# Layer 0 of a Fourier / attention transformer on one core: the gate product moved to the front, in step with a modulation that arrives in eight pieces

## The chip, the core and the metric

The kernel runs on one core of one Trainium2 chip. The metric is the device time of one execution, in microseconds. Before the change it is 1901.31 us, the median of three runs (1898.41 to 1903.77).

All weights are 32-bit floats in the chip's memory; nothing stays on the core from one execution to the next, so some 360 MB are read and written in each.

## The reference, cut to what matters

Two sequences of 256 tokens with 2048 features, `x` and `ctx`, go through two layers. The change touches only layer 0, the Fourier one, where both sequences are handled alike (in the kernel as 512 columns, 256 of each). For `x`:

```python
shift, scale, gate = split(silu(c) @ ada_w[0] + ada_b[0], 3)     # the modulation
h    = rmsnorm(x, norm_g[0]) * (1 + scale) + shift
u, z = split(h @ w_in, 2)                                        # 4096 features each
f    = fft2(u in 16 groups of 256, over tokens and within a group, ortho).real
f    = f @ w_mix[group]                                          # per group
y    = f * silu(z)                                               # gated
x    = x + gate * (y @ w_out[0])
```

For `ctx` it is the same with `c_ctx`. So there are three large products: the u product with its transforms, the z product (called the **gate product** here, since silu(z) gates f) and the **output product** y @ w_out. Layer 1 is windowed attention and a last norm; its code is the same before and after.

## The kernel before, in words

The program is written in a tile framework. Pools hand out buffers (`raw`: three of 1 MB for loaded weights; `ws`: six of 0.5 MB for split weights; `act`: 34 of 0.25 MB; eight PSUM banks of 128x512), and a scheduler fixes, at build time, the order of the instructions on each engine. On the chip each engine runs its own list in that order and waits for semaphores. Loads are issued mostly by SP, some by ScalarE (ACT) and GpSimd (POOL); a DMA issue stands in its engine's list like any instruction.

Every large product is made of three single-pass products: `split` (L59) writes the rounded high part of a 32-bit tile on ACT (L60) and the rest on VectorE (DVE, L61), and `mm3` (L72 to L75) multiplies high by high, high by low and low by high. A weight of 1 MB is loaded by `raw` (L43), split in two halves by `half_split` (L63), and used by `ws_split`'s caller.

Layer 0 has four stages:

1. **Modulation and projection** (to 140 us). `x2`, the tokens as rows, is loaded as four tiles `xn` (L152) and squared for the norm (L162). For each quarter `nb` of the features: the scale part of the modulation is made from four 1 MB tiles of `awp` in `ada_pe` (L176 to L180: four products 32x512 per tile, which leave partial sums in four strips) and `ada_fin` (L182: copy `rows`, L184; eight small products with `sel`, L187, that turn the strips into columns; L188). Behind it `xn` is normed and split (L212, L213) and projected on cosines and sines over the tokens (`dmat`; L215 to L221); `evac_hx` (L190) scales the result by the modulation and splits it into `hx`, 16 pairs. Then the shift part of the modulation comes the same way (L272 to L305), with the first Fourier group's loads, products (`u0_emit`) and `load_m(0)` placed among its tiles. The shift only enters the column of frequency 0 (`f0`, L299 to L304).
2. **Fourier groups** (to 369 us). For each of 16 groups g (L311): `load_u` (L119 to L136: weights folded by POOL at L122 and DVE at L123, then split into `wmh`, `wml`, `wph`, `wpl`), `load_m(g)` (L233 to L256: the mixing matrix `m`, loaded on ACT's queue, folded by two DVE sums, split, and ten products), 96 u products, closing products (L364) and `ft` (L369, L370). Results are written to memory as `fd`, by POOL, and by ACT in the last group. Group 0 has a side product `asp` (L340 to L350) and eight zero fills (L326).
3. **Gate product** (to 718 us). `make_hs` (L419) loads a 128-row piece of `xT` (the tokens as columns) by POOL and makes the modulated, normed h as a pair (L428, L429, L430). The first four of 32 column blocks run together (weights `wz0`), the others one by one with `wz`. `z_out` (L434) takes silu (L437) and multiplies into `y`, which has come back from `fd`. Then `next(ada)` runs one step of `ada_jobs` (L386): one tile `adw` of the modulations that are needed later, each by four to eight reductions of 512 columns on DVE (`tensor_tensor_reduce`, L400). The vector of the conditioning itself comes as `cb`, a broadcast of `crow`.
4. **Output product** (to 1057 us). 32 steps with `wo0` tiles; `y_split0` splits the next two y blocks; `evac0` (L488) adds to the residual; `ada_rate` sets how many steps of `ada` run per step.

## Time and profile before

| | |
|---|---|
| median of three runs | 1901.31 us (1898.41 to 1903.77) |
| the profiled execution | 1903.14 us |
| its span, first to last instruction | 1901.3 us |
| mean granted TensorE clock | 0.989 of full |
| TensorE busy | 1837.0 us |
| VectorE, ScalarE, GpSimd busy | 1390.1, 934.2, 236.8 us |
| memory read, written | 345.30 MB, 12.59 MB |

How to read the profile: it is one execution, and times in it count from the span's start. PE is TensorE, PEld its weight load, DVE VectorE, ACT ScalarE, POOL GpSimd, SP the engine that issues most loads. A row of the timeline has start, length, engine, line, operation, output and inputs by the program's names, shapes, count; in square brackets stands how long the engine was idle before it, and who released it. A row of the groups has count, busy time, mean ns of one, and the idle time before them. Matmuls overlap in the pipeline, so a row's length is longer than the distance to the next start; the distance is what counts. `PEclk` and "granted clock" are the share of full speed that TensorE was given.

### The profile page before, as it was taken

Reading aid. Unit: us, or ns where it says so; the run is one execution under the profiler, and the core shown is the slowest. Engines: PE = TensorE matmul, PEld = TensorE weight load, DVE = VectorE, ACT = ScalarE, POOL = GpSimd, SP = SyncE. Lnnn points to the kernel's source line nnn. Section 1 sums busy time; section 2 is a strip of 40 time slices with the busy share of each in tenths; the row PEclk is TensorE's granted clock in tenths of the full one; section 3 lists DMA queues with packets and bytes.
Section 4 is the critical chain, followed back from the end, with each engine's and each line's share of the span. In section 5 each row is a group of like instructions: output and inputs, shape, how many; then the busy total and the mean of one; then the engine's idle time right before and its main releaser. Section 6 shows DMA issues by size and latency. Waiting matters only on the chain.

```text
span 1901.3 us, 27470 instructions
## 1 busy us (share of the span) xinstructions
PE 1837.0 (97%) x10433; PEld 1585.3 (83%) x10433; DVE 1390.1 (73%) x2711; ACT 934.2 (49%) x1602; POOL 236.8 (12%) x206
## 2 busy tenths in 40 slices
PE   6879999999999999999999999999999999999997
PEld 4469999888888888888888787899989989998886
DVE  5468888788777779687985644787787777787455
ACT  3234444442222234223331434788788888887443
POOL 0033334200000000000000001102212220200001
PEclk9889999999999999999999999999999999999999
DMA  9955444646666555764577323333333333434543
GB/s 384 386 227 182 182 182 182 234 171 254 228 227 236 216 220 197 286 231 154 196 271 267 120 89 119 147 133 112 133 134 112 133 111 134 164 128 175 199 177 133
DMA packets 60532, 359.67 MB, mean 189 GB/s; under 512 B 7600, under 2 KB 7744, under 8 KB 25328
## 3 DMA queue, kind: packets, MB, share of 16 engines
q1 hardware_dynamic: 49104, 324.83, 46.1%
q0 software_dynamic: 6720, 25.34, 3.5%
q10 hardware_dynamic: 4576, 7.74, 1.1%
q8 instruction: 82, 1.34, 0.3%
q14 instruction: 50, 0.41, 0.1%
HBM read 345.30 MB, written 12.59 MB: 188 GB/s over the span
## 4 chain that ended last, share of the span: by engine, by line
PE 90%; DVE 4%; DMA 3%; issue 2%; ACT 2%; POOL 0%; ACTq 0%; POOLq 0%; DVEq 0%; SPq 0%
PE ps L74 26%; PE ps L75 26%; PE ps L73 26%; PE ps L813 3%; PE ps L828 2%; PE ps L827 2%; PE ps L794 1%; PE ps L793 1%; DMA raw<-in_awp 1%; PE ps L180 1%; DMA raw<-in_wu 1%; DVE wpl L61 1%; DMA dm<-in_dmat 0%; POOL wm L122 0%; DVE ml L61 0%
## 5 line engine op out<-in xcount | busy, mean ns | idle before, releaser
L61 DVE TENSOR_TENSOR wl<-raw,wh 128x1024 fp32r<-128x1024 f32 x333 | 423.7, 1275 | 286.7 <-ACT wh L60 284.3
L60 ACT CAST wh<-raw 128x1024 fp32r<-128x1024 f32 x333 | 349.4, 1051 | 565.4 <-PE ps L74 506.0
L74 PE MATMUL ps<-act,wh 128*128 128x512 f32 x1024 | 398.2, 389 | 0.0
L73 PE MATMUL ps<-act,wh 128*128 128x512 f32 x1024 | 394.0, 389 | 0.0
L75 PE MATMUL ps<-act,wl 128*128 128x512 f32 x1024 | 391.0, 389 | 0.0
L75 PEld LDWEIGHTS ps<-act,wl 128*128 128x128 f32 x1024 | 192.3, 188 | 39.8
L73 PEld LDWEIGHTS ps<-act,wh 128*128 128x128 f32 x1024 | 192.3, 188 | 39.8
L74 PEld LDWEIGHTS ps<-act,wh 128*128 128x128 f32 x1024 | 192.3, 188 | 39.7
L400 DVE CUSTOM_DVE_ANT_0 raw<-raw,cb 128x512 f32<-128x512 f32 x256 | 172.5, 688 | 19.8 <-DMA raw<-in_adw 15.9
L73 PE MATMUL ps<-h,wh 128*128 128x256 f32 x512 | 147.0, 287 | 0.0
L74 PE MATMUL ps<-h,wh 128*128 128x256 f32 x512 | 144.7, 283 | 0.0
L75 PE MATMUL ps<-h,wl 128*128 128x256 f32 x512 | 144.7, 283 | 0.0
L400 DVE CUSTOM_DVE_ANT_0 junk<-raw,cb 128x512 f32<-128x512 f32 x192 | 131.7, 686 | 14.2 <-ACT cb L392 7.9
L74 PE MATMUL ps<-wl,h 128*128 128x512 f32 x320 | 125.3, 391 | 1.5 <-DVE wl L61 1.5
L73 PE MATMUL ps<-wh,h 128*128 128x512 f32 x320 | 124.2, 396 | 0.4 <-ACT h L583 0.4
L75 PE MATMUL ps<-wh,h 128*128 128x512 f32 x320 | 124.5, 392 | 0.0
L122 POOL TENSOR_TENSOR wm<-raw 128x1016 f32<-128x1016 f32 x32 | 83.4, 2614 | 195.2 <-DMA raw<-in_wu 194.7
L795 DVE CUSTOM_DVE_ANT_0 ps<-ps,mask,nsink 128x512 f32<-128x512 f32 x128 | 92.0, 753 | 10.8 <-PE ps L794 10.4
L73 PEld LDWEIGHTS ps<-h,wh 128*128 128x128 f32 x512 | 97.2, 190 | 1.3
L798 ACT ACTIVATE p<-ps,mx 128x512 f32<-128x512 f32 x128 | 87.3, 687 | 21.4 <-DVE mx L795 20.4
L74 PEld LDWEIGHTS ps<-h,wh 128*128 128x128 f32 x512 | 97.4, 190 | 0.0
L75 PEld LDWEIGHTS ps<-h,wl 128*128 128x128 f32 x512 | 97.3, 190 | 0.0
(302 smaller groups left out, 3775.6 us busy)
## 6 DMA issues: line engine op xcount, KB each, us to landing
raw<-in_wz SPq DMA_DIRECT2D x64, 1024.0 KB, 4.8
raw<-in_adw SPq DMA_DIRECT2D x64, 1024.0 KB, 4.8
raw<-in_awp SPq DMA_DIRECT2D x32, 1024.0 KB, 9.2
raw<-in_wo SPq DMA_DIRECT2D x32, 1024.0 KB, 6.0
raw<-in_wq SPq DMA_DIRECT2D x32, 1024.0 KB, 4.8
raw<-in_wu SPq DMA_DIRECT2D x32, 1016.0 KB, 4.9
raw<-in_wo1b SPq DMA_DIRECT2D x16, 1024.0 KB, 4.8
act<-in_xT POOLq DMA_DIRECT2D x32, 256.0 KB, 5.3
```

Of the source, the lines that this page charges most:

```text
L60: S.copy(h, src)
L61: V.tensor_tensor(l, src, h.bitcast(F32), op=ALU.subtract)
L73: PE.matmul(o, wh, xh, start=start, stop=False)
L74: PE.matmul(o, wh, xl, start=False, stop=False)
L75: PE.matmul(o, wl, xh, start=False, stop=stop)
L122: GP.tensor_tensor(m, v[:, :, 0, :], v[:, :, 1, :], op=ALU.subtract)
L400: V.tensor_tensor_reduce(junk if s == 0 and i < 3 else wf, wf, cb[:, s, kq * 512 : kq * 512 + 512], 1.0, 0.0, ALU.mult, ALU.add, acc[:, i, ...
L795: V.tensor_tensor_reduce(o, o, mask[:, tb, :], -0.125, nsink[:, i : i + 1], ALU.add, ALU.min, mx[:, tb : tb + 1])
L798: S.activation(pt[:, tb, :], so[tb], AF.Exp, bias=mx[:, tb : tb + 1], scale=-1.0, accum_out=sm[:, tb : tb + 1])
L813: PE.transpose(o[:, (kt * 2 + tb) * P : (kt * 2 + tb + 1) * P], pt[:, tb, c : c + P], ident)
L827: PE.matmul(oo[:, 0:N], st, ph[:, q], start=kb == 0, stop=False)
L828: PE.matmul(oo[:, 0:N], st, pl[:, q], start=False, stop=kb == 3)
```

## The change

It reorders layer 0, and regroups some of its operations.

- `xT` is loaded first, as four tiles of 1 MB that stay. The norm's sums of squares come from ACT squares and products with ones.
- Scale and shift arrive in eight pieces of 256 features. `ada_tile` loads half the rows of one piece for one of the two (two transfers of 512 KB, in runs of 1 KB) and makes eight products 32x256. `ada_fin` finishes both at once.
- As soon as piece c is there, `make_hs` makes h for its two row blocks k, and seven gate blocks (`NZ`, in seven PSUM banks) accumulate over them; the four tiles of piece c+1 stand between these products.
- The other 25 gate blocks follow one by one. `z_out` only takes silu and writes the block to memory as `zd`. Behind blocks 12, 16, 20 and 24 stands one quarter of the projection (`dft`), whose scaled result stays as `dfx`; 32 of the 64 `ada` steps are placed here, with reductions of 1024 columns.
- Behind the last block: `hx` is split from `dfx`, then come the casts and loads for group 0 with its `load_m(0)` and zero fills, and 16 Fourier groups as before.
- In the output product `y_split0` loads `fd` and `zd`, multiplies them and splits; `ada_rate` is lower.

```diff
+NZ = 7
...
+    def make_hs(k, xt):
+        h, l = act(F32R), act(F32R)
+        for s in range(2):
+            q = slice(s * N, (s + 1) * N)
+            t = xt[:, q]
+            V.scalar_tensor_tensor(t, t, gs0[:, k, s : s + 1], r_bc[:, q], op0=ALU.mult, op1=ALU.mult)
+            S.activation(h[:, q], t, AF.Identity, bias=sh0[:, k, s : s + 1])
+            V.scalar_tensor_tensor(l[:, q], t, sh0[:, k, s : s + 1], h[:, q].bitcast(F32), op0=ALU.add, op1=ALU.subtract)
+        hs.append((h, l))
...
+        xts = [st.tile([P, D], F32, name=f"xt{i}") for i in range(4)]
+        for i in range(4):
+            nc.sync.dma_start(xts[i], a["xT"][:, i * 4 : (i + 1) * 4, :])
...
+        for i in range(4):
+            sq = st.tile([P, D], F32, tag="raw2", name="sq", bufs=2)
+            S.activation(sq, xts[i], AF.Square)
+            for j in range(4):
+                PE.matmul(o[j * 32 : (j + 1) * 32, :], ones32, sq[:, j * 512 : (j + 1) * 512], start=i == 0, stop=i == 3)
...
+        bcast_rows(rr, r_bc)
...
+        def ada_tile(c, w, kh):
+            t = slot_st()
+            for g in range(2):
+                src = a["awp"][1 - w, c // 2, 2 * kh + g].rearrange("p (k n) -> p k n", n=512)
+                nc.sync.dma_start(t[:, g * 1024 : (g + 1) * 1024].rearrange("p (k n) -> p k n", n=256), src[:, :, (c % 2) * 256 : (c % 2 + 1) * 256])
+            if w == 0 and kh == 0:
+                oa[c] = psum()
+            for i in range(8):
+                j = i % 4
+                PE.matmul(oa[c][j * 32 : (j + 1) * 32, w * 256 : (w + 1) * 256], c32[:, kh * 8 + i, :], t[:, i * 256 : (i + 1) * 256], start=kh == 0 and i < 4, stop=kh == 1 and i >= 4)
+
+        def ada_fin(c):
+            rows = st.tile([P, 512], F32, tag="rows", name="rows", bufs=2)
+            S.copy(rows, oa.pop(c))
             o2 = psum()
             for j in range(4):
                 PE.matmul(o2[:, j * 2 : (j + 1) * 2], rows[:, j * P : (j + 1) * P], sel, start=True, stop=True)
+            kq = slice(c * 2, c * 2 + 2)
+            o2 = o2[:, 0:8].rearrange("p (w a b) -> p w a b", w=2, b=2)
+            V.tensor_tensor(gs0[:, kq], o2[:, 0], adab[:, 0, 1, kq], op=ALU.add)
+            V.scalar_tensor_tensor(gs0[:, kq], gs0[:, kq], 1.0, ng[:, 0, kq], op0=ALU.add, op1=ALU.mult)
+            V.tensor_tensor(sh0[:, kq], o2[:, 1], adab[:, 0, 0, kq], op=ALU.add)
+
+        for w in range(2):
+            for kh in range(2):
+                ada_tile(0, w, kh)
+        ada_fin(0)
+        oz = None
+        for c in range(8):
+            wr = slot_st()
+            nc.sync.dma_start(wr[:, 0:1024], a["wz0"][c // 2][:, (c % 2) * 1024 : (c % 2 + 1) * 1024])
+            nc.sync.dma_start(wr[:, 1024:1792].rearrange("p (b n) -> p b n", b=3), a["wz"][0:3, :, c * 256 : (c + 1) * 256].rearrange("b p n -> p b n"))
...
+            for i in range(2):
+                k = c * 2 + i
+                make_hs(k, xts[k // 4][:, (k % 4) * 512 : (k % 4 + 1) * 512])
...
+                for b in range(NZ):
+                    (wh, wl), q0 = (w[0], i * 512 + b * P) if b < 4 else (w[1], (b - 4) * 256 + i * P)
+                    q = slice(q0, q0 + P)
+                    mm3(oz[b], wh[:, q], wl[:, q], hs[k][0], hs[k][1], k == 0, k == KT - 1)
+                if c < 7:
+                    for kh in range(2):
+                        ada_tile(c + 1, i, kh)
+            if c < 7:
+                ada_fin(c + 1)
...
+            def z_out(b, o):
+                z = zp.tile([P, 512], F32, tag="z", name="z")
+                S.activation(z, o, AF.Silu)
+                nc.gpsimd.dma_start(zd[b], z)
...
+            for b in range(NZ, NB):
+                w = ws_split(raw(a["wz"][b - 4]))
                 o = psum()
...
+                z_out(b, o)
+                if b in (12, 16, 20, 24):
+                    dft((b - 12) // 4)
+                if b < 29:
+                    next(ada)
+                if b in (9, 10, 14, 15, 18, 19, 22, 23, 26, 27):
+                    next(ada)
         wfp = us.enter_context(tc.tile_pool(name="wfp", reuse_waits="tile", bufs=8))
+        for k in range(KT):
+            h, l = act(F32R), act(F32R)
+            split(h, l, dfx[k])
+            hx.append((h.rearrange("p (s j) -> p s j", s=2), l.rearrange("p (s j) -> p s j", s=2)))
...
         if g == 0:
+            wsr = wsp.tile([P, 512], F32, tag="ws", name="wsr")
+            nc.scalar.dma_start(wsr, a["wsp"])
+            sph, spl = act(F32R), act(F32R)
+            split(sph, spl, wsr)
+        pqh, pql, sp = load_m(g)
...
         def y_split0(i):
             for j in range(2):
                 h, l = act(F32R), act(F32R)
-                split(h, l, ys[i % 16 * 2 + j])
+                b = i % 16 * 2 + j
+                if i < 16:
+                    z = act()
+                    nc.sync.dma_start(ys[b], fd[b])
+                    nc.sync.dma_start(z, zd[b])
+                    V.tensor_tensor(ys[b], ys[b], z, op=ALU.mult)
+                split(h, l, ys[b])
                 yy[i, j] = (h, l)
...
-        ada_rate = {2: 2, 5: 2, 8: 2, 11: 2, 15: 0, 16: 0, 19: 2, 22: 2, 25: 2, 28: 2, 30: 0, 31: 0}
+        ada_rate = {2: 2, 8: 2, 15: 0, 16: 0, 20: 2, 25: 2, 30: 0, 31: 0}
```

375 lines of the change are left out of this document (131 added, 244 removed).

## The prediction

> **What bounds the kernel now.** I read the page first: the span, the engines' busy time and the slices.
>
> ```profile
> span 1901.3 us, 27470 instructions
> PE 1837.0 (97%) x10433; PEld 1585.3 (83%) x10433; DVE 1390.1 (73%) x2711; ACT 934.2 (49%) x1602; POOL 236.8 (12%) x206
> PE   6879999999999999999999999999999999999997
> PEclk9889999999999999999999999999999999999999
> ```
>
> TensorE (PE) is the bound everywhere but in the first three slices. So a change can win only there, and whatever it adds to PE's waits later is lost in full. The windows cut the span at the stages: modulation with projection (to 140), Fourier groups 1 to 15 (to 369), gate product (to 718), output product (to 1057). Columns: length, busy time (count) of PE, PEld, DVE, ACT, POOL, granted clock, DMA share, GB/s.
>
> ```profile
> 0.00:140.00 140.00, 103.38 (x698) 67.59 (x699) 74.47 (x191) 43.89 (x83) 20.00 (x21) 0.89 0.85 339
> 140.00:369.00 229.00, 217.82 (x1779) 215.13 (x1777) 186.20 (x246) 102.59 (x191) 89.19 (x66) 1.00 0.51 189
> 369.00:718.00 349.00, 348.57 (x1544) 289.04 (x1545) 270.48 (x621) 107.99 (x144) 4.27 (x8) 1.00 0.58 219
> 718.00:1057.00 339.00, 339.00 (x1498) 280.78 (x1497) 260.21 (x595) 100.06 (x125) 10.70 (x20) 1.00 0.61 228
> ```
>
> Only the first stage has PE idle (37 us) and a low clock (0.89), with DMA at 0.85. The other three joints cost PE almost nothing: gate and output product stand at 349 of 349 and 339 of 339.
>
> The clock must be read from rows of PE in order of time, since "busy" hides it:
>
> ```profile
> 14.62 0.55 PE L73 MATMUL ps<-dh,xh 128*128 128x256 f32 x1 [5.60 <-DVE xh L212]
> 20.30 0.28 PE L74 MATMUL ps<-dl,xh 128*128 128x256 f32 x1
> 34.09 0.28 PE L74 MATMUL ps<-dl,xh 128*128 128x256 f32 x1
> 39.60 0.28 PE L75 MATMUL ps<-dh,xl 128*128 128x256 f32 x1
> 69.67 3.64 PE L180 MATMUL ps<-raw,c 128*32 128x512 f32 x32
> 74.37 1.05 PE L187 MATMUL ps<-sel,rows 128*128 128x2 f32 x8 [1.06 <-ACT rows L184]
> 75.36 1.06 PE L180 MATMUL ps<-raw,c 128*32 128x512 f32 x8
> 79.76 1.07 PE L180 MATMUL ps<-raw,c 128*32 128x512 f32 x8 [1.85 <-DMA raw<-in_awp]
> 82.83 1.94 PE L180 MATMUL ps<-raw,c 128*32 128x512 f32 x8 [2.00 <-DMA raw<-in_awp]
> 136.03 0.56 PE L364 MATMUL ps<-asp,sp 96*128 96x260 f32 x1 [5.63 <-DVE asp L350]
> 139.18 0.37 PE L244 MATMUL ps<-mh,ch 128*128 128x256 f32 x1
> ```
>
> Prices at full clock: a 256-wide product 0.12 us (46 steps from 34.09 to 39.60); a 1 MB modulation tile 0.91 us (four in 3.64); the eight `sel` products 1.05; a 512-wide product 0.226 us (the third window's 348.57 for 1544 products, of which 1536 are the gate's). After gaps everything takes about twice as long for a while (the tile at 82.83: 1.94; the 15 steps from 136.03 to 139.18 take 0.21 each). Such a restart loses 1.4 us here, 2.7 at the kernel's start (25 steps from 14.62 to 20.30 at 0.227); I take 2.2.
>
> **The change as a ledger.** I ask when PE has done the seven gate blocks (T7), and how much PE work is left then against what is left at 140.
>
> Left over: the 25 other gate blocks instead of 32, so 7 x 48 x 0.226 = 76 us less. More: the projection (192 products, 23 us), Fourier group 0 (96, 11.6 us), its side product `asp` (48, 5.8 us), two `load_m` and one closing step (34, 4.1 us): 44.5. Net 31.5 us less.
>
> T7 begins with loads. The four Squares show how 1 MB tiles land at the start:
>
> ```profile
> 10.07 1.91 ACT L162 ACTIVATE dump<-xn 128x2048 f32<-128x2048 f32 x1 [6.88 <-DMA xn<-in_x]
> 17.72 1.91 ACT L162 ACTIVATE dump<-xn 128x2048 f32<-128x2048 f32 x1 [0.48 <-DMA xn<-in_x]
> cb<-in_crow POOLq DMA_DIRECT2D x4, 1024.0 KB, 8.6
> ```
>
> MB 2 to 5 land from 10.1 to 17.7: 2.55 us each, the n-th at 4.9 + 2.55 n. Before the first piece can close, 9.9 MB come in: xT (4), the `crow` broadcast that now goes out at once (1), four modulation tiles, the first gate weights (0.9): 30.1 us. Tile 1.4, `rows` 0.75, `sel` 1.1, then `make_hs` 2.1: the first gate product starts at 35.5. The sum of squares (to about 25) and the weight split, which stands ahead of r_bc's copy on ScalarE (to 26.5), lie beside this.
>
> ```profile
> L184 ACT COPY rows<-ps 128x512 f32<-128x512 f32 x8 | 4.7, 586 | 43.7 <-PE ps L180 43.7
> 365.78 0.89 DVE L428 SCALAR_TENSOR_TENSOR act<-act,gs,r_bc 128x256 f32<-128x256 f32 x2 [4.87 <-DMA act<-in_xT]
> 366.30 0.91 ACT L429 ACTIVATE act<-act,sh 128x256 fp32r<-128x256 f32 x2 [5.07 <-DVE act L428]
> ```
>
> (0.75 is the copy with its two hand-overs; 2.1 is three small VectorE operations, two L428 and the last L429.)
>
> Each later piece costs PE 42 gate products (9.5), four tiles, the wait for `rows` 0.75, `sel` 1.05; `make_hs` is covered, because three tiles of the next piece stand between `sel` and the gate product in the built order. A tile is now 16 half-width rows instead of 8. Bounds: the same columns at the same rate, 0.91; below, nothing excludes a little less; above, 16 rows at the pace of `sel` (1.05 / 8), 2.1. The streamed columns are the same, so I go near the tile's own row: 1.1. A piece is 9.5 + 4.4 + 1.8 = 15.7 us. Seven pieces, a restart (2) and the last chain with its product (2.1 + 9.5): T7 = 35.5 + 2 + 7 x 15.7 + 11.6 = 159.
>
> Is it DMA that paces? A piece needs 4.9 MB, 12.4 us at 2.55, below 15.7: no, if runs of 1 KB (the pieces cut each row) keep the rate. The trace has none in bulk, but:
>
> ```profile
> q1 hardware_dynamic: 49104, 324.83, 46.1%
> q0 software_dynamic: 6720, 25.34, 3.5%
> q10 hardware_dynamic: 4576, 7.74, 1.1%
> ```
>
> Per percent of engine time they move 7.05, 7.24 and 7.04 MB, at 6.6, 3.8 and 1.7 KB per packet. Small runs cost nothing visible; bounds 0 and twice the time, I take 0. SP holds one `wz` load for a weight split, and the tile loads behind it have some 10 us to spare.
>
> **Joint 1, gate to Fourier** (new). After the last gate product ScalarE holds, in order: Silu z(31), the last hx cast, the wsr and ch casts, eight zero fills, and only then issues the load of `m` for load_m(0). PE's next instruction is load_m(0)'s product; all of group 0 is queued behind it, and VectorE's wml behind m's two sums.
>
> ```profile
> L437 ACT ACTIVATE z<-ps 128x512 f32<-128x512 f32 x32 | 18.9, 593 | 17.3 <-PE ps L75 17.3
> 121.11 0.51 ACT L326 ACTIVATE mh<-ident 128x128 fp32r<-128x128 f32 x2
> 121.52 0.49 ACT L326 ACTIVATE ml<-ident 128x128 fp32r<-128x128 f32 x2
> DMA to landing us min/median/max: 2.8/4.5/7.2
> 340.30 0.59 ACT L60 CAST pqh<-ps 128x512 fp32r<-128x512 f32 x1 [0.49 <-PE ps L75]
> 341.03 0.41 DVE L239 TENSOR_TENSOR mt<-m 128x256 f32<-128x256 f32 x1
> ```
>
> Four at 0.55, the eight fills 1.7 (a pair each 0.41), landing 4.5 (that row is tile m's), two sums 0.8, cast 0.6: 9.8 us. With the shortest landing, 2.8, it is 8.1. DMA is quiet then, so I take 9.3, with a restart 11.5.
>
> **Joint 2, Fourier to output product** (new: before, gate products that needed nothing from group 15 filled it, PE idle 1.06 us). VectorE has behind group 15's last sum two small splits, two reductions of modulation pieces, four sums into ft, two more reductions, then the first y*z; ScalarE's split follows and PE starts.
>
> ```profile
> 369.43 0.39 PE L73 MATMUL ps<-mh,pqh 127*128 127x256 f32 x1 [1.06 <-ACT mh L60]
> 426.35 0.68 DVE L400 CUSTOM_DVE_ANT_0 raw<-raw,cb 128x512 f32<-128x512 f32 x1
> 426.96 0.69 DVE L400 CUSTOM_DVE_ANT_0 junk<-raw,cb 128x512 f32<-128x512 f32 x1
> 405.46 2.36 DVE L61 TENSOR_TENSOR wl<-raw,wh 128x1024 fp32r<-128x1024 f32 x2 [0.46 <-ACT wh L60]
> ```
>
> A reduction, now 1024 wide, has no row: between 0.61 and twice that, 1.22; 1.15 by the 1024-wide L61 row. The splits and sums are half as wide or less, some 0.4 each by the 0.41 of `mt`, the last y*z and cast 0.6: 0.8 + 2.3 + 1.6 + 2.3 + 0.6 + 0.6 = 8.2, less 2.1 of PE's own work and of waits as before: 6, with a restart 8.
>
> **Hidden.** The projection's VectorE rows:
>
> ```profile
> L213 DVE SCALAR_TENSOR_TENSOR xl<-xn,rr,xh 128x512 fp32r<-128x512 f32 x16 | 11.2, 745 | 0.1
> L212 DVE TENSOR_SCALAR xh<-xn,rr 128x512 fp32r<-128x512 f32 x16 | 7.0, 482 | 9.5 <-PE ps L74 9.4
> ```
>
> Four projection steps now stand among gate blocks: VectorE per four blocks 9.4 (splits), 27.6 (six pieces of four reductions), 5 (four of each row) = 42 of PE's 49 us (192 products at 0.226, 48 at 0.12); it can still be late by lumps, I put 2 (bounds 0 and 8). z goes out and back (16.8 MB) where DMA stood at 0.58 and 0.61: 0. The 16 hx splits (half of the L61 row's 1.18 each on VectorE) lie beside the last block. The 5.63 wait for `asp` shrinks to under 1; one more Fourier group has the usual 0.75 of waits (229.00 less 217.82, over 15 groups): together 1.6.
>
> **Sum.** 1901.3 + (159 - 140) - 31.5 + 11.5 + 8 + 2 + 1.6 = 1912. The profiled execution took 1903.14 us, 1.8 more than its span, so 1914 by its own clock; the median 1901.31 stands 1.8 lower: 1912 again. (0.3%, 5.7 us, is what a measurement can tell from none.)
>
> **Rivals.**
> - Joints hidden (the other side): if the load of m reaches ScalarE's head before the last gate product ends, and y*z gets ahead of the reductions, PE runs through both joints as it now does at 369 and 718: minus 20, 1892. It decides at under 1 us of PE idle at each. Against: both orders are fixed at build time. Chance 0.20.
> - Pieces at the floor: tiles at 0.91 and no restart: minus 5 and 2, and if crow's load falls into a gap 2.6: 1902. Chance 0.16.
> - Cold pieces: PE gaps once per piece drop the clock, as the 1.85 and 2.00 waits did before 82.83; or tiles cost 1.6. Seven times 2.2: 1927. For: every piece has a wait on ScalarE. Against: at 74.37 a gap of 1.06 left the next tile at 1.06. Chance 0.17. [...]
> - DMA paces: 1 KB runs at half rate make a piece 22.7 us: plus 49, 1961. Chance 0.04.
> - It doesn't overlap (pieces wait for each other's loads on SP): like the former, 1930. Chance 0.03.
>
> **Numbers.** Forecast 1912 with chance 0.40 (own range 1904 to 1920). Faster comes from hidden joints and a little of the floor: 0.22. Same from the floor and the low edge of the forecast: 0.16. Slower: 0.62. The range takes in hidden joints with some of the floor and the cold pieces with a late VectorE: 1887 to 1935.
>
> **What would show it.** After: first gate product near 35, pieces 15.7 apart, T7 near 159, PE waits of about 9 and 6 us around the first load_m product and the first output product, gate blocks without waits. Wrong if T7 is under 150 or over 170, or a joint is under 3 us.

## The result, and the profile after

The changed kernel takes 1979.62 us (median of four runs, 1975.04 to 1986.77) against 1901.3: a ratio of 1.042, 95% interval 1.038 to 1.045. That is **78 us slower** (77 between the profiled executions); the forecast was 11 slower, with a range that ended at 1935. The profiled execution took 1980.45 us, its span is 1978.7, its mean granted clock 0.976 (before 0.989).

The same lines of the page as before: span, busy times, PE's slices and clock.

```profile
span 1978.7 us, 27727 instructions
PE 1861.7 (94%) x10729; PEld 1602.7 (81%) x10729; DVE 1358.1 (69%) x2203; ACT 944.2 (48%) x1617; POOL 245.6 (12%) x221
PE   5899999998899995899999999999999999999997
PEclk8899999999899998999999999999999999999999
```

PE is busy 25 us more and the span is 77 longer, so most of the loss is PE standing still. Slice 1 was low before; now a second hole stands at slice 16. The windows, cut at the new stages: front with seven gate blocks, the other gate blocks with the projection, first joint, 16 Fourier groups, second joint, output product, layer 1.

```profile
0.00:176.40 176.40, 140.65 (x953) 94.13 (x954) 57.70 (x128) 45.95 (x66) 3.02 (x12) 0.92 0.87 287
176.40:487.70 311.30, 301.62 (x1401) 251.96 (x1399) 228.33 (x353) 92.28 (x130) 23.72 (x36) 0.98 0.66 238
487.70:497.80 10.10, 0.04 (x2) 0.01 (x1) 10.10 (x13) 6.36 (x16) 2.91 (x2) 0.71 0.18 52
497.80:751.50 253.70, 243.77 (x1968) 240.88 (x1968) 209.88 (x276) 113.62 (x208) 92.49 (x59) 0.98 0.53 191
751.50:767.00 15.50, 0.02 (x1) 0.02 (x1) 6.73 (x14) 0.94 (x3) 0.00 (x0) 0.61 0.58 213
767.00:1148.70 381.70, 362.76 (x1577) 296.18 (x1577) 260.49 (x389) 116.10 (x151) 11.41 (x21) 0.98 0.60 222
1148.70:1978.70 830.00, 812.80 (x4832) 719.49 (x4832) 584.87 (x1034) 568.96 (x1045) 112.07 (x91) 0.99 0.39 138
```

These are PE's long waits, from the timeline after (in brackets: idle before, and released by whom):

```profile
37.28 2.72 PE L74 MATMUL ps<-act,wh 128*128 128x512 f32 x7 [1.99 <-ACT act L187]
59.36 5.35 PE L230 MATMUL ps<-raw,c 128*32 128x256 f32 x48 [4.24 <-issue]
166.87 0.47 PE L74 MATMUL ps<-act,wh 128*128 128x512 f32 x1 [2.36 <-DVE gs L241]
250.84 1.23 PE L74 MATMUL ps<-dh,xh 128*128 128x256 f32 x4 [7.30 <-ACT dh L61]
343.11 0.50 PE L74 MATMUL ps<-act,wh 128*128 128x512 f32 x1 [1.85 <-ACT wh L61]
497.79 0.58 PE L74 MATMUL ps<-mh,ch 128*128 128x256 f32 x1 [10.06 <-ACT mh L61]
766.98 3.35 PE L74 MATMUL ps<-act,wh 128*128 128x512 f32 x7 [15.51 <-ACT act L61]
794.89 3.78 PE L74 MATMUL ps<-act,wh 128*128 128x512 f32 x8 [7.23 <-ACT act L61]
```

The output product in the trace of before, for comparison, with its end: no wait at all in 354.1 us.

```profile
718.50:1072.60 354.10, 353.90 (x1582) 293.55 (x1580) 273.70 (x619) 110.11 (x141) 11.22 (x21) 1.00 0.59 220
```

So the forecast's ledger can be filled in, term by term:

| term (us against before) | forecast | measured | how measured |
|---|---|---|---|
| seven blocks done | +19 | +36.4 | 176.4 - 140 |
| work left behind them | -31.5 | -31.5 | same count of products |
| waits in gate blocks and projection | +2 | +17.1 | 311.3 - (1200 x 0.226 + 192 x 0.12) |
| first joint | +11.5 | +10.1 | its wait; its slow clock is in the next row |
| 16 Fourier groups, extra waits | +1.6 | +2.0 | what is left of the sum |
| second joint | +8 | +14.4 | 15.5 - 1.06 |
| output product | 0 | +27.6 | 381.7 - 354.1 |
| layer 1 | 0 | +1.3 | 830.0 - (1901.3 - 1072.6) |
| sum | +10.6 | +77.4 | 1978.7 - 1901.3 |

Four terms are off: output product, front, gate blocks, second joint. (The +2.0 of the Fourier groups is near its forecast, but not by the forecast's parts: the wait for `asp`, put at under 1 us, was 3.31.) The experiments go by these. The changed kernel itself varies by 12 us from run to run, so effects of 5 us were read from the stages of the profiled execution, not from the time; the stages are given as lengths. They vary too: in the runs below that leave it alone the output product took 374 to 386 us, and the Fourier groups 254 to 260. The wait at the first joint, by contrast, came back to 0.01 us (10.05 or 10.06) wherever nothing near it was changed.

### The profile page after: what moved, and what is told of

Its sections match the earlier page's. It is cut to its first block, busy times and chain, and to the rows that moved or that the text cites. A ratio compares the mean times of both kernels' runs of the same rounds, so it can differ in the third digit from the quotient of the medians.

```text
span 1978.7 us, 27727 instructions
## 1 busy us (share of the span) xinstructions
PE 1861.7 (94%) x10729; PEld 1602.7 (81%) x10729; DVE 1358.1 (69%) x2203; ACT 944.2 (48%) x1617; POOL 245.6 (12%) x221
## 4 chain that ended last, share of the span: by engine, by line
PE 69%; issue 11%; DVE 6%; DMA 4%; ACT 2%; POOL 1%; POOLq 0%; ACTq 0%; SPq 0%; DVEq 0%
PE ps L75 20%; PE ps L74 20%; PE ps L76 20%; PE ps L785 3%; PE ps L800 2%; PE ps L799 1%; PE ps L766 1%; PE ps L765 1%; DMA raw<-in_adw 1%; DMA cb<-in_crow 1%; DVE wl L62 1%; DVE junk L164 1%; DMA raw<-in_wu 1%; DVE raw L164 1%; ACT wh L61 1%
## 5 line engine op out<-in xcount | busy, mean ns | idle before, releaser
L74 PE MATMUL ps<-act,wh 128*128 128x512 f32 x1024 | 364.7, 401 | 41.7 <-ACT act L61 34.1
L75 PE MATMUL ps<-act,wh 128*128 128x512 f32 x1024 | 402.2, 393 | 0.1
L76 PE MATMUL ps<-act,wl 128*128 128x512 f32 x1024 | 400.2, 392 | 0.5 <-DVE wl L62 0.5
L74 PEld LDWEIGHTS ps<-act,wh 128*128 128x128 f32 x1024 | 195.8, 193 | 91.2 <-ACT act L61 39.0
L75 PEld LDWEIGHTS ps<-act,wh 128*128 128x128 f32 x1024 | 194.3, 190 | 43.5 <-DVE act L188 1.2
L164 DVE CUSTOM_DVE_ANT_0 raw<-raw,cb 128x1024 f32<-128x1024 f32 x128 | 155.2, 1222 | 34.8 <-DMA raw<-in_adw 33.4
L164 DVE CUSTOM_DVE_ANT_0 junk<-raw,cb 128x1024 f32<-128x1024 f32 x96 | 117.3, 1222 | 47.3 <-DMA raw<-in_adw 36.0
L76 PE MATMUL ps<-wh,h 128*128 128x512 f32 x320 | 124.6, 392 | 0.0
```

What stands on the lines that cost most here:

```text
L74: PE.matmul(o, wh, xh, start=start, stop=False)
L75: PE.matmul(o, wh, xl, start=False, stop=False)
L76: PE.matmul(o, wl, xh, start=False, stop=stop)
L164: V.tensor_tensor_reduce(junk if s == 0 and i < 3 else wf, wf, cb[:, s], 1.0, 0.0, ALU.mult, ALU.add, acc[:, i, kh, fg * 2 + f, s : s + 1])
```

## The experiments

### First four: each cause as the trace first suggests it

At the second joint the timeline of VectorE and SP reads:

```profile
755.04 1.23 DVE L164 CUSTOM_DVE_ANT_0 raw<-raw,cb 128x1024 f32<-128x1024 f32 x1 [4.74 <-DMA raw<-in_adw]
758.07 7.13 SPq L450 DMA_DIRECT2D y<-fd  x7
763.29 1.23 DVE L164 CUSTOM_DVE_ANT_0 raw<-raw,cb 128x1024 f32<-128x1024 f32 x1 [4.54 <-DMA raw<-in_adw]
765.59 0.69 DVE L452 TENSOR_TENSOR y<-y,act 128x512 f32<-128x512 f32 x1
```

VectorE stands for two `adw` tiles ahead of the last `ft` and the first y*z, and from 758 on SP issues all 32 loads of `fd` (until 785.8) with few others between. My theory was a **queue**: that burst, ahead of `zd` and `wo0`, delays the output product.

**e1_pace**: fd and zd loads tied to the weight tile ahead.

```diff
-                    nc.sync.dma_start(ys[b], fd[b])
-                    nc.sync.dma_start(z, zd[b])
+                    with tc.issue_after(last_dma[0]):
+                        nc.sync.dma_start(ys[b], fd[b])
+                        nc.sync.dma_start(z, zd[b])
```

> Each pair of y and z loads of the output product is issued only behind the weight tile of the step ahead. Theory (queue): after the change all 32 loads of fd, 8 MB, stand on SP in one burst ahead of zd and wo0, and this makes PE's eight later waits in the output product (17.8 us, and slow clock behind each). So they fall to under 6 us, the first wait (15.5) stays within 4 us, and the time falls by 14 to 25 us, to some 1955 to 1965. Rival (reductions): VectorE's list, not SP's, is what is late; its list is nearly the same here, so the time falls by less than 4 us. Rival (traffic): z's trip through memory itself is too much for the DMA engines; then pacing moves the waits to other places, with the same sum.

Measured: 1988.66 us, ratio 1.044 (1.042 to 1.047). The 7.23 wait at the start went, but waits of 5.0, 3.7, 3.3 and 6.2 came at 834 to 914; the output product took 393.5. The queue theory fell: the burst can be spread and nothing is won.

**e2_noada**: no modulation jobs in the first four output steps, two in each of eight later ones.

```diff
-        ada_rate = {2: 2, 8: 2, 15: 0, 16: 0, 20: 2, 25: 2, 30: 0, 31: 0}
+        ada_rate = {0: 0, 1: 0, 2: 0, 3: 0, 6: 2, 8: 2, 10: 2, 12: 2, 15: 0, 16: 0, 20: 2, 22: 2, 24: 2, 26: 2, 30: 0, 31: 0}
```

> The first four steps of the output product carry no modulation jobs; eight later steps carry two. Theory (queue): of the first wait of 15.5 us the two waits of VectorE for adw tiles (4.74 and 4.54) and two pairs of reductions (4.6) go, it falls to some 5 us; the burst of fd loads stays, so the later waits stay at 12 us or more; the time falls by 8 to 16 us. Rival (reductions): VectorE's own load is the cause of first and later waits; both go and the time falls by 28 us or more. Rival (SP): fd loads can't start before the Fourier buffers are free, so y is late with or without reductions: the first wait stays above 11.

```profile
755.18 3.46 PE L74 MATMUL ps<-act,wh 128*128 128x512 f32 x8 [2.66 <-ACT act L61]
```

```profile
755.18:1147.50 392.32, 367.69 (x1577) 298.00 (x1577) 268.96 (x405) 116.04 (x151) 11.42 (x21) 0.97 0.61 226
```

The second joint's wait fell from 15.5 to 2.66, as the theory had it: the jobs made it. But the time was 1978.95, no change, because the output product grew from 382 to 392: the long wait at its start stayed (7.55 at 786), and waits of 1.81 and 3.48 came at 856 and 873, among the steps with two jobs. What is taken from the joint comes back in the steps.

**e3_dm**: the cosine table loaded and split before the single gate blocks.

```diff
-                if nb == 0:
-                    dm = zp.tile([P, 2, N], F32, tag="z", name="dm")
-                    nc.gpsimd.dma_start(dm, a["dmat"])
-                    split(dh, dl, dm)
...
+        dm = act().rearrange("p (a b) -> p a b", a=2)
+        nc.gpsimd.dma_start(dm, a["dmat"])
+        split(dh, dl, dm)
```

> The cosine table dm is loaded and split ahead of the single gate blocks, in a buffer of its own. Theory: the 7.30 us wait at the first projection step is the load of dm, issued by GpSimd behind the second broadcast of crow, and its cast, queued on ScalarE behind the silu of that broadcast; with the table there early the wait goes, and with it the slow clock behind it: minus 8 to 11 us. Rival: ScalarE is held by the silu of cb until 247 us anyway, and what PE needs next (weight casts) is behind it: the wait only moves by a few us, minus 0 to 4.

```profile
250.24 0.50 PE L74 MATMUL ps<-act,wh 128*128 128x512 f32 x1 [1.42 <-ACT wh L61]
492.04 0.58 PE L74 MATMUL ps<-mh,ch 128*128 128x256 f32 x1 [10.06 <-ACT mh L61]
```

The 7.30 wait is gone, a wait of 1.4 for a weight cast stands in its place, and the first joint ends 5.8 us earlier (492.04 for 497.79). The time was 1982.44: the Fourier groups (257.4 for 253.7) and the output product (385.7 behind 765.27) took that back within their own spread. So this names the cause of some 6 of the 17 us in the gate blocks, and shows no gain in the time.

**e4_awp**: the modulation weights laid out by pieces, so that runs are 4 KB.

```diff
-                src = a["awp"][1 - w, c // 2, 2 * kh + g].rearrange("p (k n) -> p k n", n=512)
-                nc.sync.dma_start(t[:, g * 1024 : (g + 1) * 1024].rearrange("p (k n) -> p k n", n=256), src[:, :, (c % 2) * 256 : (c % 2 + 1) * 256])
+                q = slice(g * 1024, (g + 1) * 1024)
+                nc.sync.dma_start(t[:, q], a["awp"][1 - w, c, kh][:, q])
```

> The modulation weights lie in memory piece by piece, so that their transfers have runs of 4 KB instead of 1 KB; same bytes, same number of transfers, same order on every engine but for what the scheduler moves. Theory (short runs): the pieces' first three periods (19.8, 22.4, 18.1 us) are long because transfers of 1 KB runs move some 20% slower than others; they fall to 17, the first gate product comes 1 to 2 us earlier, and the time falls by 6 to 13 us. Rival (clock and hand-overs, the cold pieces of the prediction): periods are made on PE, ScalarE and VectorE; they stay and the time changes by under 3 us.

Measured: 1983.73 us. The periods sum to 125.7 (129.2 before the edit, 126.1 in e1_pace, which left the runs at 1 KB), and the first gate product came at 38.4, not earlier. Short runs are not the cause, as the forecast had assumed.

### Next four: other engines for the suspects

Within the output product's first sweep the trace shows a loop that lasts 11.4 us (two rounds from 904.64 to 927.49) where PE's step is 10.85. VectorE and SP in the changed kernel:

```profile
897.59 1.23 DVE L164 CUSTOM_DVE_ANT_0 junk<-raw,cb 128x1024 f32<-128x1024 f32 x1 [1.12 <-DMA raw<-in_adw]
902.78 0.69 DVE L452 TENSOR_TENSOR y<-y,act 128x512 f32<-128x512 f32 x1 [0.40 <-DMA act<-zd]
903.39 1.22 DVE L164 CUSTOM_DVE_ANT_0 raw<-raw,cb 128x1024 f32<-128x1024 f32 x1
904.64 0.33 SPq L47 DMA_DIRECT2D raw<-in_adw  x1
909.50 1.22 DVE L164 CUSTOM_DVE_ANT_0 junk<-raw,cb 128x1024 f32<-128x1024 f32 x1 [1.17 <-DMA raw<-in_adw]
```

The `adw` tile's four reductions have a weight split and a y*z between them; only behind the last (903.39 to 904.5) is the buffer free; SP then loads the next (904.64), VectorE waits for it at 909.50. Load 4.9 plus list 6.5. That was the second theory, the **loop**.

**e5_pool**: half of the low parts of hx on GpSimd.

```diff
-            split(h, l, dfx[k])
+            S.copy(h, dfx[k])
+            (GP if k % 2 else V).tensor_tensor(l, dfx[k], h.bitcast(F32), op=ALU.subtract)
```

> The low halves of eight of the sixteen hx pairs are made by GpSimd instead of VectorE, nothing else. Theory (backlog): the 10.06 us wait of the first Fourier product is VectorE's backlog of hx splits (13 of 0.65 us from 481 to 496 without a pause, since hx can only take the buffers that hs gives back during the last gate block), with ScalarE's zero fills and m's sums behind it. Half of it gone, the wait falls to between 3 and 6.5 us. Rival (the prediction's chain): ScalarE's list, which issues the load of m last, and that load's landing make the wait; it stays at 9 to 10.5.

```profile
481.00 12.20 DVE L124 TENSOR_TENSOR raw<-raw 128x1016 f32<-128x1016 f32 x1
481.06 3.79 POOL L339 TENSOR_TENSOR act<-dfx,act 128x512 fp32r<-128x512 f32 x3
484.81 2.39 POOL L123 TENSOR_TENSOR wm<-raw 128x1016 f32<-128x1016 f32 x1
487.17 4.95 POOL L339 TENSOR_TENSOR act<-dfx,act 128x512 fp32r<-128x512 f32 x4
504.84 0.58 PE L74 MATMUL ps<-mh,ch 128*128 128x256 f32 x1 [15.92 <-ACT mh L61]
```

Neither number came: the wait grew to 15.92. One VectorE sum that takes 1.2 us elsewhere took 12.20 while GpSimd ran eight operations in a row (481.1 to 492.1), and ended 1.1 behind that run. So VectorE's backlog grew by 11 instead of shrinking, and PE's wait grew by 6. The edit failed as a remedy, but VectorE's list grew longer, and PE's wait with it: that speaks for VectorE, and against m's load, as what the joint waits for. Time 1982.91 (ratio 1.040 to 1.046).

**e8_bothpool**: loads of fd and zd issued by GpSimd (`nc.sync` to `nc.gpsimd` in both lines of y_split0).

> The loads of fd and zd for the output product are issued by GpSimd instead of SP. Theory (queue): wo0 and adw tiles no longer stand behind 8 MB of fd, so the waits of 1.43, 7.23 and 2.76 us in the first 75 us of the output product shrink to a third; the steady 1.5 us per step behind 862 us stay; time from the first output product to the sums of squares behind the last 382 to some 367. Rival (loop): all waits of the first sweep come from the loop of one raw buffer: adw's load (4.9), four reductions with a split and y*z between them (6.5), next load; then loads on another queue change under 4 us.

Measured: 2002.9 us; output product 401.5, with a first wait of 18.4 and then 14.0. Another queue for the same 16 MB makes it worse: GpSimd issues nearly all of `fd` first (until 783.5), all but one load of `zd` behind it.

**e9_mulpool**: y*z on GpSimd.

```diff
-                    V.tensor_tensor(ys[b], ys[b], z, op=ALU.mult)
+                    GP.tensor_tensor(ys[b], ys[b], z, op=ALU.mult)
```

> The product y*z of the output stage is made by GpSimd instead of VectorE; loads as in the changed kernel. Theory (loop): in the first sweep a step lasts 11.5 instead of 10.85 us because adw's buffer goes round in load 4.9 plus 6.5 of VectorE's list; without y*z in that list it is near 10.2 and PE is the bound again, so that the steady waits behind 862 us (1.5 per step) go: 8 to 12 us less in the output product. Rival (queue): the waits come from SP's list alone and stay. In both cases the burst's waits ahead of 850 stay.

Measured: 1987.58 us; output product 390.1. The products take 1.8 us there (mean from 860 to 955 us), and VectorE's reductions beside them 1.42 and 1.52 on average instead of 1.22, single ones 2.3; so nothing could be learned of the loop from it.

**e12_both_mul**: both edits.

> Both edits: loads of fd and zd by GpSimd, and y*z on GpSimd. If queue and loop are separate causes, their gains add up: the output product takes 382 less 20 to 27 us, near the 354 of before. If GpSimd's own list becomes the bound (each z waits for the load ahead of it, a product takes 1.3 us and stands among the issues), it gains less than either alone.

Measured: 1994.51 us; output product 401.2. No gain adds up.

### Then four that take work away

**x1_noz**: z neither loaded nor multiplied in the output stage.

```diff
-                    z = act()
...
-                    nc.sync.dma_start(z, zd[b])
-                    V.tensor_tensor(ys[b], ys[b], z, op=ALU.mult)
```

> Leaves out the gating: the output product takes f itself, z is neither loaded nor multiplied (it is still computed and written). Theory (adw's buffer loop): with y*z and the waits for zd out of VectorE's list the loop of adw's buffer falls from 11.5 to some 10 us, PE is the bound in the first sweep, and the output product falls from 382 to 362 to 370 us; the first wait (15.5), which adw's landings make, stays above 10. Rival (z's trip): the loads of zd and their place on SP are the whole cost of the output stage; then the first wait goes as well and the stage takes 354 to 358.

```profile
764.43:1119.09 354.66, 354.46 (x1577) 293.93 (x1577) 240.94 (x360) 115.24 (x151) 11.39 (x21) 1.00 0.59 218
```

Measured: 1951.27 us. The output product takes 354.7, what it took before, although all 32 loads of `fd` still come in one burst, and the first wait stays at 14.1. So z's return makes 27.0 of the +27.6, and the burst of `fd` by itself costs nothing; the second joint is a cause of its own.

**x3_narrow**: reductions of three modulation pieces over 64 columns.

```diff
+                                n = 1024 if i == 0 else 64
-                                V.tensor_tensor_reduce(junk if s == 0 and i < 3 else wf, wf, cb[:, s], 1.0, 0.0, ALU.mult, ALU.add, acc[:, i, kh, fg * 2 + f, s : s + 1])
+                                V.tensor_tensor_reduce((junk if s == 0 and i < 3 else wf)[:, 0:n], wf[:, 0:n], cb[:, s, 0:n], 1.0, 0.0, ALU.mult, ALU.add, acc[:, i, kh, fg * 2 + f, s : s + 1])
```

> The reductions of the modulation pieces 1 to 3 are done over 64 columns instead of 1024, so those pieces are not complete; all loads stay. Theory (adw's buffer loop): the loop is load 4.9 plus what VectorE does until the last reduction; with 0.1 us reductions the buffer is free soon after the load, so the steady waits go; of the first wait the two landings stay partly. Output product 382 to 356 to 368 us, and the whole 25 us or more shorter in the output stage. Rival (queue and burst): the fd burst and zd's place on SP make the waits; then it stays above 374.

```profile
760.32:1130.43 370.11, 360.49 (x1577) 297.53 (x1577) 178.06 (x389) 115.47 (x151) 11.40 (x21) 0.97 0.61 226
```

Measured: 1963.19 us. With 82 us less on VectorE the steady waits behind 860 are gone, but 5.8 and 3.6 stay at 780 and 829: 370, two us over what the loop theory allowed. Long reductions make some 12 of the 27.6 (the stage's own spread is 374 to 386); the rest stays with z's loads.

**e14_pair**: the last two gate blocks by halves.

```diff
+            for kh in range(2):
+                for i in range(2):
+                    wh, wl = half_split(rz[i], kh)
+                    for j in range(8):
+                        k = kh * 8 + j
+                        q = slice(j * P, (j + 1) * P)
+                        mm3(oz[i], wh[:, q], wl[:, q], hs[k][0], hs[k][1], k == 0, k == KT - 1)
```

> The last two gate blocks run by halves (rows 0 to 7 of both, then 8 to 15 of both), so the first eight pairs of hs are free 10.8 us ahead of the stage's end instead of 5.4. Nothing is left out. Theory (backlog): the 10.06 us wait ahead of load_m(0) is VectorE working off 16 hx splits that must wait for hs's buffers; the wait falls to between 3 and 7. Rival (ScalarE's list and m's landing): it stays at 9 to 10.5.

```profile
491.84 0.58 PE L74 MATMUL ps<-mh,ch 128*128 128x256 f32 x1 [7.02 <-ACT mh L61]
```

The wait fell from 10.06 to 7.02, just past the edge of what the backlog theory allowed, and far outside the rival's. Time 1978.91 (ratio 1.036 to 1.047).

**x4_half**: tiles of the modulation load half their rows and use them twice.

```diff
-            for g in range(2):
+            for g in range(1):
...
-                PE.matmul(oa[c][j * 32 : (j + 1) * 32, w * 256 : (w + 1) * 256], c32[:, kh * 8 + i, :], t[:, i * 256 : (i + 1) * 256], start=kh == 0 and i < 4, stop=kh == 1 and i >= 4)
+                PE.matmul(oa[c][j * 32 : (j + 1) * 32, w * 256 : (w + 1) * 256], c32[:, kh * 8 + i, :], t[:, j * 256 : (j + 1) * 256], start=kh == 0 and i < 4, stop=kh == 1 and i >= 4)
```

> Each modulation tile loads half of its rows and uses them twice, so that modulation is made of half its weights; products and orders stay. Theory (loads pace the pieces): a piece of 4.9 MB at the 340 GB/s that the trace shows in its busy stretches takes 15.1 us, and SP can't run ahead of five buffers, so loads make the first pieces late (the 4.24 us wait) and the clock low behind it; with 2.9 MB the first gate product comes 5 to 7 us earlier and the sum of the seven periods falls from 129 to 114 to 119. Rival (hand-overs): the periods are made of PE, ScalarE and VectorE handing over; the start moves, but the seven periods sum to 122 or more.

Measured: 1980.09 us. The seven periods sum to 132.4, the first gate product came later (43.7), and a wait of 3.29 for a tile stays at 65 us. The late start is not the modulation loads' doing: in this build the second weight split, which waits for its own tile until 39.98, stands ahead of the first `make_hs` (42.20), and PE waits 7.71 there instead of 1.99. Without that difference the periods sum to 126.6, within the 124.6 to 129.4 of the runs that leave the front alone. With two fifths less to load nothing shows as faster, so bytes alone don't hold the front; a gain of a few us can't be excluded.

### Last six: can z stand elsewhere, and do the causes add up

**f1_slots**: six buffers in the front's ring (`raw2` with bufs=3, `cnt[0] % 6`).

> The front's ring has six buffers of 1 MB instead of five (three of the kind raw2). Theory (buffer round trip): a piece needs five buffers, they come free only behind PE's gate products of the piece ahead, so SP stands and the first tile of the next piece lands late (4.24 us wait, slow clock behind it); with a sixth buffer the seven periods sum to 115 to 123 instead of 129 and PE's wait for a tile near 59 us falls under 1.5. Rival (hand-overs and the clock): 126 or more.

Measured: 1987.23 us. The wait for a tile near 59 is gone, and the periods sum to 123.5, just past the theory's 123. With six buffers they sum to 122.2 to 123.5 (here, f4_all and x6_floor), with five to 124.6 to 129.4: the ring costs 1 to 6 of the 17 us. Behind it, waits of 9.6 (for `dh`) and 4.4 in the gate blocks took it back.

**f2_zf**: z multiplied into f in the Fourier groups; the output product reads only the product.

```diff
             S.copy(ft[:, :, 128:129], gcv[:, :, 128:129])
+            z = act()
+            nc.sync.dma_start(z, zd[g * 2 + db])
+            fz = ft.rearrange("p s j -> p (s j)")
+            V.tensor_tensor(fz, fz, z, op=ALU.mult)
```

> z is loaded back and multiplied into f in each Fourier group, on VectorE, and only the product is written and read by the output product. Nothing is left out. Theory (z in the output stage is what costs): the output product takes 354 to 358 as without z, the first wait stays at 12 to 16, and the Fourier groups, where VectorE is at 0.72, take 0 to 8 more: 1979 to some 1955 to 1962. Rival (VectorE in the Fourier groups has no room where it counts, at each group's end): the groups take 15 us or more longer and half the gain is lost.

```profile
494.08:767.80 273.72, 251.26 (x1968) 247.36 (x1968) 242.81 (x307) 114.18 (x208) 90.46 (x59) 0.96 0.57 206
767.80:1127.90 360.10, 355.92 (x1578) 294.87 (x1577) 247.14 (x372) 115.97 (x155) 11.43 (x21) 0.99 0.60 222
```

Measured: 1960.72 us, ratio 1.032 (1.030 to 1.034). The output product is back at 356, the second joint at 4.0 (not 12 to 16, as I had expected), and the 16 Fourier groups take 273.7 instead of 253.7: the waits for `ml` at each group's end grew from at most 1.2 to up to 2.9, with slow clock behind some (the first product behind the 2.92 at 601.29 took 0.58 for 0.39; the stage's granted clock is 0.96 for 0.98). z costs 20 there instead of 27 (f3_zf_rate and f4_all, with the same groups, have 282.3 and 274.5).

**f3_zf_rate**: f2_zf with the rates of e2_noada.

> As f2_zf, and the first four output steps carry no modulation jobs, eight later steps two. Theory: the second joint's wait falls from some 14 to 3 (as in e2_noada), and now that z is out of the loop the doubled steps cost less than 5: 10 us less than f2_zf. Rival (the loop of one adw buffer, 4.9 load and 4.9 reductions and a split, fills a step alone): each doubled step costs 5 or more us and the gain is lost, as in e2_noada.

Measured: 1964.74 us: nothing was left to win at the joint (3.5 for 4.0), and the Fourier groups took 282.3 for 273.7 with the same code. But the output product with its doubled steps took 355, like f2_zf's 356 without them. So the doubled steps cost nothing once z is out of the stage, as the theory had it: what e2_noada paid, it paid for the jobs together with z.

**f4_all**: f3_zf_rate with e3_dm, e14_pair and f1_slots.

> f3_zf_rate with the early cosine table (e3_dm), the paired last gate blocks (e14_pair) and six buffers (f1_slots). If the named causes are the whole, the stages add up: front minus 8, gate blocks minus 6, first joint minus 3, second joint and output minus 35: 1979 to some 1925 to 1935, so still slower than before; if something else paces the kernel, less than 40 us come back.

Measured: 1954.46 us, ratio 1.028 (1.026 to 1.030): 25 us back, the best complete version, and half of what I had added up; z's 20 us in the Fourier groups are most of the gap.

**x5_znarrow**: y*z over 32 columns, loads of z as in the changed kernel.

```diff
-                    V.tensor_tensor(ys[b], ys[b], z, op=ALU.mult)
+                    V.tensor_tensor(ys[b][:, 0:32], ys[b][:, 0:32], z[:, 0:32], op=ALU.mult)
```

> The product y*z in the output stage is done over 32 of 512 columns, so the rest of f stays ungated; all loads of z and the wait for them stay. Theory (loads and their waits in VectorE's list): the output product stays at 372 or more. Rival (VectorE's time, 0.6 us per product in a list that is full): it falls to 364 or less.

```profile
761.73:1138.95 377.22, 360.43 (x1577) 296.46 (x1577) 244.19 (x389) 116.94 (x151) 11.41 (x21) 0.97 0.61 225
```

The output product stays at 377. Of z's 27 us, 22.5 remain with loads and waits alone; the products' own 4.5 isn't clear of the stage's spread. VectorE stands in its list for z seven times, 19.0 us in all, and all behind it stands too. Time 1972.12.

**x6_floor**: x1_noz with e2_noada, e3_dm, e14_pair and f1_slots.

> z's product left out of the output stage (the output product takes f ungated), with the early cosine table, the paired last blocks, six buffers in the front and no modulation jobs in the first four output steps. If the named causes are the whole: output product near 355, second joint under 4, first joint 7, front and gate blocks some 8 less than the changed kernel: 1979 to some 1922 to 1932, still above before, since the front's seven blocks save no more than the work that is put behind them. Rival (another cause): above 1938.

```profile
0.00:169.70 169.70, 138.41 (x960) 94.98 (x961) 58.52 (x131) 47.44 (x68) 3.59 (x13) 0.93 0.91 300
169.70:476.90 307.20, 300.26 (x1394) 250.69 (x1392) 230.73 (x355) 91.67 (x129) 23.36 (x35) 0.98 0.66 240
483.90:743.80 259.90, 244.75 (x1968) 241.29 (x1968) 208.42 (x269) 113.43 (x208) 89.90 (x59) 0.98 0.49 180
```

Measured: 1934.45 us, ratio 1.016 (1.012 to 1.021), between what I expected (to 1932) and the rival (from 1938). Even with z for nothing the kernel is slower than before: the front ends at 169.7, so 29.7 - 31.5, a gain of 2 us, and the gate blocks (13 over their pure length), the first joint (7) and the Fourier groups (8 over before's pace with group 0's work) stand against it.

## Why the prediction was wrong, step by step

**The sign was right, the size was off by a factor of seven, and the likeliest case fell with its range.** The sign had its reason in part: the two joints cost 24.5 us, where I had 19.5. But front and moved work together, forecast as 12.5 gained, came to 4.9 lost, and the largest loss is one that I had at nothing. By its own steps:

- **Output product, forecast 0: the step that failed.** I wrote that z goes out and back where DMA stood at 0.58 and 0.61, and priced that at nothing. It cost 27.6, and 27.0 of that go with z's return (x1_noz). The bandwidth was there, as I said; the price is in the order. Before, the product of f and z stood in the gate stage, where `fd` was loaded beside each weight tile and no product waited for it. Now each z has to land in the middle of VectorE's list (it stood for z eight times, 12.7 us in all), between reductions that hold the buffer that SP needs next. Loads with their waits are 22.5 of it (x5_znarrow); with short reductions 16 are left (x3_narrow), and without z doubled reductions cost nothing (f3_zf_rate): the two act on each other and don't add up. How much of it is VectorE standing and how much SP's buffers isn't separated. Without this term the kernel still takes 1951 (x1_noz), past the range's end, so the steps below failed on their own account.
- **Seven blocks done, forecast 159, measured 176.4.** The first gate product came at 37.3 (forecast 35.5). The tile's 1.1 was right: in the fast pieces four took 4.4. But a fast piece lasted 16.8, not 15.7: behind `sel` PE waits a second time (0.37), `make_hs` isn't quite covered (0.38), and the 42 gate products, cut up by tiles, take 10.0 instead of 9.5. That is some 7.5 in seven. Five pieces lasted 17.2 to 22.4, together 11.6 more than fast ones, where I had a restart of 2 (another 2.0 is the first piece's own wait for `make_hs`, which the forecast has in its start). This is the ring of five buffers, where I gave the tile loads "some 10 us to spare" and PE waited 4.24 (f1_slots: 1 to 6 of it), and the clock.
- **Cold pieces** had a chance of 0.17 and came in some pieces only. In the changed kernel nearly the same run of tile products (46 and 42) took 4.30 or 2.75, behind the same waits of 0.7 and 0.37:

```profile
77.89 4.30 PE L230 MATMUL ps<-raw,c 128*32 128x256 f32 x46 [0.37 <-PE ps L237]
131.28 2.75 PE L230 MATMUL ps<-raw,c 128*32 128x256 f32 x42 [0.37 <-PE ps L237]
```

```profile
77.00:81.00 4.00, 3.63 (x45) 2.51 (x47) 2.85 (x8) 1.89 (x4) 0.00 (x0) 0.75 0.96 319
79.00:82.41 3.41, 3.41 (x31) 1.77 (x24) 2.85 (x6) 2.65 (x5) 0.00 (x0) 0.50 1.05 358
130.00:134.00 4.00, 3.63 (x50) 2.48 (x50) 2.46 (x8) 1.50 (x3) 0.00 (x0) 1.00 0.97 308
```

- The granted clock is 0.75 in the one and 1.00 in the other. I had leaned on one row where a gap of 1.06 left the clock alone. The traces show which pieces are hit. In the changed kernel's the low clock (0.50) comes in stretches of 3.41 us or multiples of it, and these start on one grid: 58.52, 79.00, 96.07 and 167.75 us lie 6, 5 and 21 times 3.41 apart. Between two pieces PE has, for 2.1 us, nothing but two waits and the eight `sel` products. At 75.76 these 2.1 us lie wholly in one stretch of the grid (75.59 to 79.00), and the next stretch is slow (0.50 to 82.41); at 129.17 the grid cuts them at 130.20 into 1.03 and 1.08, and the clock stays (1.00). The traces of the changed kernel and of the 18 runs made from it have 98 such places: the clock fell behind all 36 that have 1.95 us or more in one stretch, behind none of the 57 that have at most 1.88, and behind three of the five between. In the trace of before, where slow stretches start at 81.34 and 98.41 (5 times 3.41 apart), the same spacing cuts the row that I had leaned on (74.37) at 74.51: that it kept its clock was luck, and in these traces a cold piece is a matter of where the grid falls.
- **Gate blocks, forecast 2, measured 17.1.** "Late by lumps" had bounds of 0 and 8. The lumps were a load that I had not followed: GpSimd issues `dm` behind the second broadcast of `crow`, and ScalarE's cast of it stands behind the silu of that broadcast: 7.3 (e3_dm), and 2.4 for a weight tile whose buffer an `adw` tile held; of the rest, some 7, the slow clock behind these waits explains about 4.5 (half speed until 256.5, and from 345.2 to 348.7); some 3 stay untraced.
- **First joint, forecast 9.3, measured 10.1: near by luck, since the chain was another.** Not m's late issue alone: VectorE, which still splits hx, goes from these splits to `mt`, the first sum over m, without a pause.

```profile
489.06 6.14 DVE L62 TENSOR_TENSOR act<-dfx,act 128x512 fp32r<-128x512 f32 x6
492.83 0.51 ACT L388 ACTIVATE mh<-ident 128x128 fp32r<-128x128 f32 x2 [2.88 <-DVE act L62]
493.45 0.33 ACTq L346 DMA_DIRECT2D m<-in_wm  x1
496.33 0.41 DVE L350 TENSOR_TENSOR mt<-m 128x256 f32<-128x256 f32 x1
```

In e14_pair m was sent for well ahead (485.21), and `mt` still began only when VectorE got to it:

```profile
485.21 0.33 ACTq L357 DMA_DIRECT2D m<-in_wm  x1
490.39 0.41 DVE L361 TENSOR_TENSOR mt<-m 128x256 f32<-128x256 f32 x1
```

- I had hidden those 16 splits beside the last block. They don't all fit there: hx takes the buffers that hs frees, and hs is read to the end of that block, so six were left at its end. One of the six took 3.13 us beside a GpSimd sum of 2.35. e14_pair and e5_pool moved the wait both ways with VectorE's list. (That the fills wait because their pool lies where `dfx` lay is argued, not shown.)
- **Second joint, forecast 6 and a restart, measured 15.5.** The order that I had read was right. I priced the reductions (1.15 each; measured 1.15 from start to start) and forgot that each pair waits for its tile: 4.74 and 4.54, which with the 6 make 15.4. Without these jobs the wait is 2.66 (e2_noada).
- **Pacing by DMA** (0.04) and **no overlap** (0.03) were rightly small; 1 KB runs cost no time that shows (e4_awp: periods of 125.7 without them, 129.2 and 126.1 with them). **Joints hidden** (0.20) was wrong at both joints.

What stays open: whether the 3 to 6 us that e3_dm, e14_pair and f1_slots gain in their stage are really lost again further on. The stages behind them are longer by that much, but no run separates this from the stages' own spread. In the two runs that have all three, the Fourier groups do begin 9 to 14 us earlier (488.5 in f4_all and 483.9 in x6_floor, for 497.8).

## What to carry to other kernels

When a product is moved to another stage, ask in which engine's list its operand will have to land, and what stands behind it there; free bandwidth says nothing about that (DMA stood at 0.60 in the output product, which still cost 27.6 us more). A list that takes 10 of 11 us on paper was over-full here once it held two waits for loads (1.12 and 0.40 us around 900: a round of 11.4 where PE's step is 10.85), and a job in it that holds a shared buffer until its last instruction adds the load's latency to the round (4.9 to the list's 6.5). Buffers that pass from one stage to the next (hs to hx, `dfx` to the Fourier pools) make joints, and each joint cost a chain (10.1 and 15.5 us) and a clock restart (0.50 until 4.5 and 4.9 us behind its first product), so that filling one hole with later work dug others.

## What the hardware showed that I had not expected

VectorE was held up strongly beside GpSimd: a two-input VectorE sum of 1.2 us took 12.20 beside a run of GpSimd operations (e5_pool), and VectorE's reductions rose from 1.22 to 1.42 and 1.52 on average with single GpSimd products of 1.8 us beside them (e9_mulpool). In e5_pool the sum lasted not through one GpSimd operation but through eight in a row (481.06 to 492.12), and ended 1.1 us behind them. What holds it there, no run shows.

In these traces TensorE's slow stretches start on one grid of 3.41 us: behind some 2 us without large products the next stretch had half the clock (0.50) when 1.95 us or more of them lay in one stretch (36 places of 36), and kept it when at most 1.88 us did (57 of 57). The same loop was therefore fast in one repetition and slow in the next (2.75 and 4.30 us for nearly the same tile products).
